# A two-layer hybrid trunk on one core: the recurrence's preparation in small pieces, a staging pool on the other side of memory, two right sides per step

## The chip, the cores and the metric

One core of one Trainium2 chip. The metric is the device time in microseconds of one execution. The engines are TensorE (PE; its weight loads are listed as PEld), VectorE (DVE), ScalarE (ACT), GpSimd (POOL) and SyncE (SP), which here only issues DMAs.

## The reference

Two layers over 1024 tokens of width 1024. Each is a token mixer, an MLP and a gated per-layer input, each behind an RMSNorm and added to the residual. The mixer of layer 0 is attention; that of layer 1 a recurrence (S5, complex and diagonal, 32 groups of 16 channels with 64 states) beside a short convolution. Cut to what matters here:

```python
for i in range(DEPTH):                          # DEPTH = 2
    hn = rms_norm(h, norm_mix[i])
    y = attention_mixer(hn, ...) if i % 2 == 0 else recurrent_conv_mixer(hn, ...)   # ends in "@ w_out"
    h = h + y
    hn = rms_norm(h, norm_mlp[i])
    h = h + jnp.square(jax.nn.relu(hn @ w_mlp_in[i])) @ w_mlp_out[i]    # 1024 -> 4096 -> 1024
    hn = rms_norm(h, norm_ple[i])
    h = h + (p[i] @ w_ple_proj[i]) * jax.nn.sigmoid(hn @ w_ple_gate[i])
return rms_norm(h, norm_final)

# in s5_mixer, from the parameters alone (the kernel's "preparation"):
abar_re, abar_im = mag * jnp.cos(li * dt), mag * jnp.sin(li * dt)
bb_re = coef_re[..., None] * br - coef_im[..., None] * bi
```

## The kernel before

**Products.** Every fp32 operand is split into a high part (ScalarE, L76) and the rest, the low part (VectorE, L79 for data, L89 for weights). `mm3` (L93) makes three matmuls of a product: L95 high × high, L96 low data × high weights (the names in the trace say `xl,wh`), L97 high data × low weights. `wtile` (L81) loads a raw block of weights `wr` (two buffers) on SP's queue and splits it into `wh` and `wl` (three buffers each). A matmul has 512 columns, half of the tokens.

**Order.** TensorE's instructions stand in the order of the program. On the other engines a scheduler sets the order by the program's order; each engine then works through its own row of instructions, and SP issues its DMAs one after the other.

**Layer 0's MLP up** (`mlp_up_plain`, L356). 32 blocks m of the hidden width, two halves n each, 24 matmuls a half. The first two blocks run together. When the first result is to be evicted, `rstd_full` makes the norm's scale from the statistics: its sums are two more matmul groups, copied out by VectorE as `rs_v` (L137). Then `out` (L361) evicts each half, scaled, into a tile `z` (VectorE, L370), and behind a full block ScalarE applies Relu and Square (L375, L376). For each pair of blocks `z_out` (L633) makes differences `tt` on VectorE (L642 to L645) and stores `z` (`oa`, `ob`, issued by ScalarE, L639, L640) and `tt` (`ot`, issued by GpSimd, L647) to the chip's memory. `z` and `tt` lie in a pool `cu`, on the left side of the on-chip memory.

**The recurrence's preparation** (`s5_prep`, a generator) needs only parameters, so it runs inside these 32 blocks, a piece at each of nine values of m:

```python
if m in (1, 5, 9, 12, 16, 19, 22, 25, 27):
    next(prep, None)
```

The first `next` runs the whole introduction (exponentials, sine and cosine, powers: many small VectorE operations on 128x32) and the first of eight "quads" (`s5_quad`: four groups each; products `Gt` and `CA`, tables `ct` and `st`). What a quad has for TensorE, four transposes (L1131) and four small matmuls, sits in `later`, run at the `next` after.

**Layer 0's MLP down** (`mlp_down`) opens a pool on the left, in the place where `cu` was. Its loads `raw` (weights, L668) and `zr` (the stored `z`, L674) alternate on SP's queue, and are split into `wh`, `wl`, `zh`, `zl`. The very first product is a lead (`down_lead`, operands `sh`, `sl`), loaded and split inside MLP up.

**Layer 1's output projection** (`out_proj_halves`, L409) runs left and right halves of the tokens apart, eight blocks m each. In the right half, at m = 1 and m = 2, four of the left half's rows of blocks each are normed (L465) and split (L79 into `x0l` to `x7l`): the right sides of the MLP that follows.

Of the kernel before, what the change touches and what calls it, by code (L numbers as in the profile page):

```python
# [13 lines left out]
ALU = mybir.AluOpType  # L14
# [51 lines left out]
class Trunk:  # L66
# [95 lines left out]
    def run(self):  # L162
        tc, nc, A = self.tc, self.nc, self.A
        pool = tc.tile_pool
        with pool(name="w", bufs=1, side=LEFT) as self.wp, \
# [11 lines left out]
            for l in range(2):  # L177
                if l == 0:
                    self.attention(xp)
                with pool(name=f"md{l}", bufs=6, space=PSUM, reuse_waits="tile") as self.mx, ExitStack() as rs:  # L180
# [4 lines left out]
                    if l == 0:  # L185
                        with pool(name=f"xu{l}", bufs=1, side=RIGHT, reuse_waits="tile") as xu:
                            hp = hs.enter_context(pool(name=f"h{l}", bufs=1, side=RIGHT, reuse_waits="tile"))
                            sp = self.ss.enter_context(pool(name=f"st{l}", bufs=1, side=RIGHT, reuse_waits="tile"))
                            xs, st = self.out_proj(l, xp, hp, xu, sp)
                            nxt.close()  # L190
                            with pool(name=f"cu{l}", bufs=1, side=LEFT, reuse_waits="tile") as cu:
                                first = self.mlp_up_plain(l, xs, st, cu, xu, hs)
# [163 lines left out]
    def mlp_up_plain(self, l, xs, st, cu, xu, hs):  # L356
# [5 lines left out]
        def out(m, n, ps):  # L362
            if not r:
                r.append(self.rstd_full(st, xu, cu))
                self.ss.close()
                hs.close()
            s = slice(n * H, n * H + H)
            if m not in z:
                z[m] = cu.tile([P, T], F32, tag="zp", bufs=4, name="z")
            nc.vector.tensor_tensor(z[m][:, s], ps, r[0][:, s], ALU.mult)  # L370
            if n:
                if m == FB - 1:
                    with self.tc.high_priority():
                        first.append(self.down_lead(l, self.s0))
                nc.scalar.activation(z[m], z[m], AF.Relu)  # L375
                nc.scalar.activation(z[m], z[m], AF.Square)  # L376
                if m % 2:
                    self.z_out(m // 2, z.pop(m - 1), z.pop(m), cu)
                if m in (1, 5, 9, 12, 16, 19, 22, 25, 27):
                    next(prep, None)  # L380

        with self.tc.tile_pool(name=f"s0{l}", bufs=1, side=LEFT, reuse_waits="tile") as self.s0:
# [26 lines left out]
    def out_proj_halves(self, l, xp, hp, sp, xa, X):  # L409
# [35 lines left out]
        for s in (lt, rt):  # L445
            for m in range(3 if s is lt else 0, KB):
# [8 lines left out]
                if s is rt and m in (1, 2):  # L455
                    for k in range(m * 4 - 4, m * 4):
                        self.norm_half(l, h, st, k, lt)
                        X[m, k % 4] = self.split(h[k][:, lt], xa, (f"x{k}h", f"x{k}l"), 1)
# [502 lines left out]
    def s5_prep(self):  # L961
# [4 lines left out]
        with tc.tile_pool(name="prep", bufs=1, side=LEFT, reuse_waits="tile") as pr:  # L966
# [16 lines left out]
            self.pexp(dt, ld, tmp)  # L983
            x = tmp()
            v.tensor_tensor(x, lr, dt, ALU.mult)
            self.pexp(mag, x, tmp)
            x = tmp()
            v.tensor_tensor(x, li, dt, ALU.mult)
            self.sincos(sn, cs, x, tmp)

# [19 lines left out]
            for t in range(8):  # L1010
                for j in range(2):
                    nc.scalar.copy(rv[j][:, t * G : (t + 1) * G], w(j, 7 - t))

# [14 lines left out]
            v.tensor_tensor(ci, ci, den, ALU.mult)  # L1028

# [16 lines left out]
            pend = None  # L1046
            for q in range(8):
                if pend:
                    pend()
                pend = self.s5_quad(q, pr, pw, rv, cr, ci, rot, sgn, nsgn)  # L1050
                yield
            pend()
# [11 lines left out]
    def s5_quad(self, q, pr, pw, rv, cr, ci, rot, sgn, nsgn):  # L1064
# [21 lines left out]

        def outer(out, tab, nt, X1, X2):
# [9 lines left out]
        outer(Gt, rv, 8, bb1, bb2)  # L1097
        CA = big("CA", 576)
        outer(CA, pw, 9, C1, C2)
        ca4 = CA.rearrange("p (g t c) -> p g t c", g=4, c=16)  # L1100
        cc = big("cc")
        nc.scalar.copy(cc.rearrange("p (g t c) -> p g t c", g=4, c=16), ca4[:, :, 1:9, :])
        self.spill(pr, q, 4, cc)

# [4 lines left out]
        for j in range(7):  # L1109
# [9 lines left out]
            v.tensor_tensor(s3[:, :, hi], s3[:, :, hi], m, ALU.add)  # L1119
        v.tensor_scalar(st, st, sgn, None, ALU.mult)  # L1120
# [3 lines left out]
        def later():  # L1124
            ps = self.bank()
            for g in range(4):
                nc.tensor.transpose(ps[:, g * P : g * P + P], Gt[:, g * P : g * P + P], self.ident)
            self.spill(pr, q, 2, ps)
            kp = self.bank()
            for g in range(4):  # L1130
                nc.tensor.matmul(kp[0:16, g * P : g * P + P], bb1[:, g * 16 : g * 16 + 16], ca4[:, g, 0:8, :], start=True, stop=True)  # L1131
            M = big("M")
            v.memset(M, 0.0)
            kt = big("kt")[0:16]
            nc.scalar.copy(kt, kp[0:16, :])
            k4 = kt.rearrange("p (g t c) -> p g t c", g=4, c=16)
            di = pr.tile([16, 64], F32, name="di", tag="di", bufs=1)
            v.tensor_tensor(g4(di), self.ident[0:16, 0:16].unsqueeze(1).to_broadcast([16, 4, 16]),
                            self.s5_dT[:, gs].unsqueeze(2).to_broadcast([16, 4, 16]), ALU.mult)
            v.tensor_tensor(k4[:, :, 0, :], k4[:, :, 0, :], g4(di), ALU.add)  # L1140
            m4 = M.rearrange("p (g t c) -> p g t c", g=4, c=16)
            for t in range(8):
                nc.sync.dma_start(m4[t * 16 : t * 16 + 16, :, t:8, :], k4[:, :, 0 : 8 - t, :])
            self.spill(pr, q, 0, M)
        return later
# [961 lines left out]
```

## Time and profile before

| | |
|---|---|
| median of three runs | 2575.11 us (2574.72 to 2578.71) |
| the profiled execution | 2579.28 us |
| its span in the trace | 2577.5 us |
| TensorE busy | 2486.7 us, 96% |
| VectorE busy | 1726.0 us, 67% |
| ScalarE busy | 1082.6 us, 42% |
| granted TensorE clock, mean | 0.985 |

The profiled execution is one of its own, apart from the three timed runs. All starts below are in microseconds from the start of its span. TensorE's share is high enough that the kernel's time is TensorE's work and the gaps in it. The clock is given in parts of 2.4 GHz.

### The profile page before, as it was taken

How to read it: one execution, taken by the hardware profiler on the slowest of the kernel's cores; microseconds unless marked ns; L12 is line 12 of the kernel's file. 1: busy time of each engine (PE TensorE's matmuls, PEld its weight loads, DVE VectorE, ACT ScalarE, POOL GpSimd, SP SyncE). 2: the span in 40 equal slices, each digit the busy share in tenths (PEclk: the TensorE clock that was granted, in tenths of full speed). 3: DMA queues.
4: the chain of work that ended last, by engine and by line, in shares of the span. 5: the costliest groups of instructions: out<-in, count | busy, mean ns of one | idle time of the engine just before them, and what ended most of it. 6: DMA issues, size and time to landing. Idle time of an engine off the chain costs nothing.

```text
span 2577.5 us, 33019 instructions
## 1 busy us (share of the span) xinstructions
PE 2486.7 (96%) x12104; PEld 2057.1 (80%) x12104; DVE 1726.0 (67%) x3189; ACT 1082.6 (42%) x1615; POOL 131.3 (5%) x128
## 2 busy tenths in 40 slices
PE   8999999979899999899999999999899999999998
PEld 6888898968687877688887897887688887888877
DVE  6776756554766776356776768665786664568776
ACT  5554555542333333343344432333554444333445
POOL 1111111000000000000000000000000000000000
PEclk9999999989999999999999999999999999999999
DMA  5443524264254555677853656354353447677552
GB/s 175 111 131 97 150 63 118 61 198 154 85 180 164 197 190 193 270 239 242 282 191 134 212 171 194 131 187 132 139 196 135 152 170 297 235 243 280 202 183 97
DMA packets 184754, 449.82 MB, mean 175 GB/s; under 512 B 24848, under 2 KB 56848, under 8 KB 184592
## 3 DMA queue, kind: packets, MB, share of 16 engines
q1 hardware_dynamic: 155904, 371.94, 43.8%
q0 software_dynamic: 12800, 46.14, 4.6%
q10 hardware_dynamic: 15888, 29.63, 3.1%
q8 instruction: 95, 1.56, 0.3%
q14 instruction: 67, 0.55, 0.1%
HBM read 297.55 MB, written 123.73 MB: 163 GB/s over the span
## 4 chain that ended last, share of the span: by engine, by line
PE 85%; DVE 8%; ACT 2%; issue 2%; DMA 1%; SPq 0%; DVEq 0%; ACTq 0%
PE mm L95 26%; PE mm L97 26%; PE mm L96 26%; PE tp L1927 2%; PE S L1894 1%; PE S L1895 1%; PE o L1952 1%; PE o L1951 1%; DVE zl L79 1%; DVE p L1897 1%; PE S L2019 1%; DVE wl L89 0%; DVE h L465 0%; DVE tl L79 0%; DVE p L1916 0%
## 5 line engine op out<-in xcount | busy, mean ns | idle before, releaser
L97 PE MATMUL mm<-xh,wl 128*128 128x512 f32 (+1 forms) x1504 | 583.9, 388 | 13.4 <-DVE st L1108 8.7
L95 PE MATMUL mm<-xh,wh 128*128 128x512 f32 (+1 forms) x1504 | 589.9, 392 | 0.3 <-ACT wh L76 0.3
L96 PE MATMUL mm<-xl,wh 128*128 128x512 f32 (+1 forms) x1504 | 580.8, 386 | 1.6 <-DVE xl L155 1.6
L95 PE MATMUL mm<-zh,wh 128*128 128x512 f32 x880 | 350.2, 398 | 8.5 <-ACT zh L76 8.5
L96 PE MATMUL mm<-zl,wh 128*128 128x512 f32 x880 | 350.1, 398 | 1.7 <-DVE zl L79 1.7
L97 PE MATMUL mm<-zh,wl 128*128 128x512 f32 x880 | 349.8, 397 | 0.0
L97 PEld LDWEIGHTS mm<-xh,wl 128*128 128x128 f32 x1504 | 284.5, 189 | 78.2 <-DVE st L1108 9.1
L96 PEld LDWEIGHTS mm<-xl,wh 128*128 128x128 f32 x1504 | 284.7, 189 | 61.4 <-DVE xl L155 2.0
L95 PEld LDWEIGHTS mm<-xh,wh 128*128 128x128 f32 x1504 | 284.6, 189 | 59.8 <-ACT sph L76 1.5
L76 ACT ACTIVATE wh<-wr 128x1024 fp32r<-128x1024 f32 (+1 forms) x137 | 143.8, 1052 | 446.1 <-PE mm L96 356.1
L95 PEld LDWEIGHTS mm<-zh,wh 128*128 128x128 f32 x880 | 166.4, 189 | 49.9 <-ACT zh L76 9.3
L96 PEld LDWEIGHTS mm<-zl,wh 128*128 128x128 f32 x880 | 166.4, 189 | 43.0 <-DVE zl L79 2.5
L97 PEld LDWEIGHTS mm<-zh,wl 128*128 128x128 f32 x880 | 166.3, 189 | 40.5
L76 ACT ACTIVATE wh<-raw 128x1024 fp32r<-128x1024 f32 x78 | 82.7, 1060 | 239.9 <-issue 117.0
L79 DVE TENSOR_TENSOR wl<-raw,wh 128x1024 fp32r<-128x1024 f32 x78 | 95.4, 1223 | 100.3 <-ACT wh L76 100.2
L89 DVE TENSOR_TENSOR wl<-wr,wh 128x1024 fp32r<-128x1024 f32 x98 | 119.6, 1222 | 59.6 <-ACT wh L76 59.3
L1902 ACT ACTIVATE p<-p,m 128x128 f32<-128x128 f32 (+7 forms) x128 | 99.1, 774 | 96.6 <-DVE m L1897 95.5
L79 DVE TENSOR_TENSOR zl<-zr,zh 128x1024 fp32r<-128x1024 f32 x110 | 134.1, 1219 | 2.4 <-ACT zh L76 2.2
L76 ACT ACTIVATE zh<-zr 128x1024 fp32r<-128x1024 f32 x110 | 115.0, 1045 | 0.7 <-DMA zr<-oa 0.7
L95 PE MATMUL mm<-wh,xh 128*128 128x256 f32 x384 | 112.6, 293 | 2.1 <-DVE v L1651 1.4
L97 PE MATMUL mm<-wh,xl 128*128 128x256 f32 x384 | 109.7, 286 | 0.0
L96 PE MATMUL mm<-wl,xh 128*128 128x256 f32 x384 | 109.6, 285 | 0.0
(680 smaller groups left out, 4476.2 us busy)
## 6 DMA issues: line engine op xcount, KB each, us to landing
raw<-w_m SPq DMA_DIRECT2D x158, 512.0 KB, 5.8
wr<-w_m SPq DMA_DIRECT2D x69, 512.0 KB, 4.1
ot<-tt POOLq DMA_DIRECT2D x64, 512.0 KB, 5.0
zr<-ot SPq DMA_DIRECT2D x64, 512.0 KB, 4.9
ob<-z ACTq DMA_DIRECT2D x32, 512.0 KB, 4.6
zr<-ob SPq DMA_DIRECT2D x32, 512.0 KB, 4.2
s<-s SPq DMA_DIRECT2D x64, 256.0 KB, 5.0
wr<-w_out SPq DMA_DIRECT2D x24, 512.0 KB, 3.5
```

The lines of the kernel that those rows point to most:

```text
L76: self.nc.scalar.activation(out, in_, AF.Copy, scale=scale)
L79: self.nc.vector.tensor_tensor(out, full, hi.bitcast(F32), ALU.subtract)
L89: self.weng.tensor_tensor(l, raw, h.bitcast(F32), ALU.subtract)
L95: mm(ps, L[0], R[0], start=first, stop=False)
L96: mm(ps, L[0], R[1], start=False, stop=False)
L97: mm(ps, L[1], R[0], start=False, stop=last)
L1894: nc.tensor.matmul(S, qh, qk["k"][c][:, k], start=True, stop=False)
L1895: nc.tensor.matmul(S, ql, qk["k"][c][:, k], start=False, stop=True)
L1897: nc.vector.tensor_tensor_reduce(pt[:, k], S, self.tab[:, T - w + k.start : T - w + k.stop], -0.125, m, ALU.add, ALU.min, m2)
L1902: nc.scalar.activation(pt[:, :w], pt[:, :w], AF.Exp, bias=m, scale=-1.0, accum_out=den)
L1927: nc.tensor.transpose(tps[:, off + n * P : off + n * P + P], maps[j][:, kb * P : kb * P + P], self.ident)
L1951: nc.tensor.matmul(oq, vv, th[:, q], start=first, stop=False)
```

## The change

Three edits, independent in the code.

1. `s5_prep` and `s5_quad` yield in 78 places: six in the introduction, nine in a quad. `out` calls `next` once behind the left and twice behind the right half of every block from m = 1. The quads' parts for TensorE now stand at m = 5, 8, 11, ... 26 (before: 5, 9, 12, ... 27), in the line of the quad itself.
2. The pool `cu` opens on the right side, behind the statistics, once the pools of the statistics (`st`) and of the residual (`h`) are closed; the temporaries of `rstd_full` go to the pool `s0` on the left.
3. In `out_proj_halves` two norms and splits stand at each of m = 1, 2, 3, 4.

```diff
-                            with pool(name=f"cu{l}", bufs=1, side=LEFT, reuse_waits="tile") as cu:
-                                first = self.mlp_up_plain(l, xs, st, cu, xu, hs)
+                            first = self.mlp_up_plain(l, xs, st, xu, hs)
...
-    def mlp_up_plain(self, l, xs, st, cu, xu, hs):
+    def mlp_up_plain(self, l, xs, st, xu, hs):
...
-                r.append(self.rstd_full(st, xu, cu))
+                r.append(self.rstd_full(st, xu, self.s0))
                 self.ss.close()
                 hs.close()
+                r.append(cs.enter_context(self.tc.tile_pool(name=f"cu{l}", bufs=1, side=RIGHT, reuse_waits="tile")))
+            cu = r[1]
...
-                if m in (1, 5, 9, 12, 16, 19, 22, 25, 27):
+            if m:
+                for _ in range(1 + n):
                     next(prep, None)
 
-        with self.tc.tile_pool(name=f"s0{l}", bufs=1, side=LEFT, reuse_waits="tile") as self.s0:
+        with self.tc.tile_pool(name=f"s0{l}", bufs=1, side=LEFT, reuse_waits="tile") as self.s0, ExitStack() as cs:
...
-                if s is rt and m in (1, 2):
-                    for k in range(m * 4 - 4, m * 4):
+                if s is rt and m in (1, 2, 3, 4):
+                    for k in range(m * 2 - 2, m * 2):
                         self.norm_half(l, h, st, k, lt)
-                        X[m, k % 4] = self.split(h[k][:, lt], xa, (f"x{k}h", f"x{k}l"), 1)
+                        X[k // 4 + 1, k % 4] = self.split(h[k][:, lt], xa, (f"x{k}h", f"x{k}l"), 1)
...
             self.pexp(dt, ld, tmp)
+            yield
             x = tmp()
             v.tensor_tensor(x, lr, dt, ALU.mult)
             self.pexp(mag, x, tmp)
+            yield
...
-            pend = None
+            yield
             for q in range(8):
-                if pend:
-                    pend()
-                pend = self.s5_quad(q, pr, pw, rv, cr, ci, rot, sgn, nsgn)
-                yield
-            pend()
+                yield from self.s5_quad(q, pr, pw, rv, cr, ci, rot, sgn, nsgn)
...
         outer(Gt, rv, 8, bb1, bb2)
+        yield
         CA = big("CA", 576)
         outer(CA, pw, 9, C1, C2)
+        yield
...
         self.spill(pr, q, 4, cc)
+        yield
...
+            if j in (2, 4):
+                yield
...
-        def later():
-            ps = self.bank()
-            for g in range(4):
-                nc.tensor.transpose(ps[:, g * P : g * P + P], Gt[:, g * P : g * P + P], self.ident)
-            self.spill(pr, q, 2, ps)
...
+        yield
+        ps = self.bank()
+        for g in range(4):
+            nc.tensor.transpose(ps[:, g * P : g * P + P], Gt[:, g * P : g * P + P], self.ident)
+        self.spill(pr, q, 2, ps)
+        kp = self.bank()
...
+        yield
+        M = big("M")
```

Lines of the changed kernel lie one or two further down from MLP up on, and more behind the new yields. Where instructions stand, at three places:

VectorE, layer 0's MLP up, around the low weights (L89) of blocks 3 and 4, before. `CA`, `ct`, `st`, `spl`, `om`, `rm` belong to the first quad, `rc` and `rs_76..` to the introduction; the two `rs_v` of the norm stand 63 and 61 rows ahead of the first L89:

```order
L1095 TENSOR_TENSOR CA<-CA,om 128x576
L1038 TENSOR_TENSOR rc_7670<-rc_7663 128x32
L1041 SCALAR_TENSOR_TENSOR rs_7671<-rc_7663,rs_7664 128x32
L1107 MEMSET ct 128x4
L1040 TENSOR_TENSOR rc_7670<-rc_7670,tiny 128x32
L370 TENSOR_TENSOR z<-mm,rstd 128x512
L1114 TENSOR_TENSOR ct<-ct,rc_7628 128x4
L370 TENSOR_TENSOR z<-mm,rstd 128x512
L79 TENSOR_TENSOR spl<-cc,sph 128x512
L89 TENSOR_TENSOR wl<-wr,wh 128x1024
L1108 MEMSET st 128x4
```

The same engine with the change:

```order
L1088 TENSOR_TENSOR bb_7780<-bb_7780,bc 128x64
L1047 TENSOR_TENSOR rc_7703<-rc_7703,tiny 128x32
L1046 TENSOR_TENSOR tiny<-rs_7704 128x32
L89 TENSOR_TENSOR wl<-wr,wh 128x1024
L137 TENSOR_SCALAR rs_v<-mm 128x512
L1045 TENSOR_TENSOR rc_7710<-rc_7703 128x32
L1048 SCALAR_TENSOR_TENSOR rs_7711<-rc_7703,rs_7704 128x32
L137 TENSOR_SCALAR rs_v<-mm 128x512
L1047 TENSOR_TENSOR rc_7710<-rc_7710,tiny 128x32
L1046 TENSOR_TENSOR tiny<-rs_7711 128x32
```

The first L89 has gone from behind the evictions and the first quad's `CA` to the row ahead of the first `rs_v`, in the middle of the introduction; the second L89 stands 35 rows behind that `rs_v`.

SP, from the last load of the gate's weights (`w_pg`) into the first loads of layer 0's MLP down, with the semaphores that each issue waits for, before. DMAHW5 of the first `raw` is the store of the last `ob`, its DVE the last `tt`, its Activation the last Square; DMASW are the stores of `ot`, issued by GpSimd:

```order
L83 DMA wr<-w_pg 128x1024 [waits DMAHW2_49,DVE_49]
L668 DMA raw<-w_m 128x1024 [waits DMAHW5_49,DMAHW6_49,DVE_49,Activation_49]
L674 DMA zr<-oa_184 128x1024 [waits DMAHW7_49]
L668 DMA raw<-w_m 128x1024 [waits DMASW7_49,DMASW5_49,DMAHW0_49,DMASW3_49,DMASW1_49]
L674 DMA zr<-oa_185 128x1024 [waits DMAHW1_49,PE_49]
```

With the change (DMAHW6 of the first `raw` is the `ob` store of block 27, its PE a matmul of the norm's statistics; DMAHW0 of the second a load of `w_pg`; the first `zr` waits for transfers and a matmul of the last quad):

```order
L83 DMA wr<-w_pg 128x1024 [waits DMAHW5_49,DMAHW2_49,DVE_49]
L670 DMA raw<-w_m 128x1024 [waits DMAHW6_49,PE_49]
L676 DMA zr<-oa_184 128x1024 [waits DMAHW3_49,DMAHW7_49,DMAHW1_49,PE_49]
L670 DMA raw<-w_m 128x1024 [waits DMAHW0_49]
L676 DMA zr<-oa_185 128x1024 [waits DMAHW4_49,DMAHW1_49]
```

The first `raw` no longer waits for the last `ob`, for VectorE or for ScalarE, and the second no longer for `ot`.

VectorE, layer 1's output projection, right half, from an eviction (L426) to the low weights (L89) of block 4, before:

```order
L426 TENSOR_TENSOR h<-mm,h 128x512
L79 TENSOR_TENSOR x4l<-h,x4h 128x512
L465 SCALAR_TENSOR_TENSOR h<-h,gains,rstd 128x512
L434 TENSOR_TENSOR acc<-acc,sq 128x512
L465 SCALAR_TENSOR_TENSOR h<-h,gains,rstd 128x512
L79 TENSOR_TENSOR x5l<-h,x5h 128x512
L465 SCALAR_TENSOR_TENSOR h<-h,gains,rstd 128x512
L79 TENSOR_TENSOR x6l<-h,x6h 128x512
L426 TENSOR_TENSOR h<-mm,h 128x512
L79 TENSOR_TENSOR x7l<-h,x7h 128x512
L89 TENSOR_TENSOR wl<-wr,wh 128x1024
```

With the change, the rows up to the same L89 (L428 is the eviction, L467 the norm, L436 the statistics):

```order
L467 SCALAR_TENSOR_TENSOR h<-h,gains,rstd 128x512 x3
L428 TENSOR_TENSOR h<-mm,h 128x512
L79 TENSOR_TENSOR x2l<-h,x2h 128x512
L79 TENSOR_TENSOR x3l<-h,x3h 128x512
L436 TENSOR_TENSOR acc<-acc,sq 128x512
L79 TENSOR_TENSOR x4l<-h,x4h 128x512
L467 SCALAR_TENSOR_TENSOR h<-h,gains,rstd 128x512
L89 TENSOR_TENSOR wl<-wr,wh 128x1024
```

The low weights of block 4 stand behind `x4l` now, no longer behind `x7l`: six rows fewer from the first eviction of the right half.

## Rows read from the trace of the kernel before

**Rows 1.** The page: its first line, and in part 1 the engines' busy time.

```profile
span 2577.5 us, 33019 instructions
...
PE 2486.7 (96%) x12104; PEld 2057.1 (80%) x12104; DVE 1726.0 (67%) x3189; ACT 1082.6 (42%) x1615; POOL 131.3 (5%) x128
```

**Rows 2.** Waits of TensorE: engine, line, what ended them, us in all, times, longest.

```profile
PE mm L97 <- DVE st L1108: 8.7, 1, 8.7
...
PE mm L95 <- ACT zh L76: 8.5, 2, 8.2
```

**Rows 3.** Windows: us, busy of PE, PEld, DVE, ACT, POOL; PE clock, DMA share, GB/s.

```profile
700.00:720.00 20.00, 14.81 (x53) 11.83 (x54) 18.66 (x74) 6.54 (x7) 0.00 (x0) 0.74 0.61 205
800.00:900.00 100.00, 100.00 (x440) 80.09 (x439) 73.18 (x233) 34.44 (x40) 5.80 (x8) 1.00 0.54 185
```

**Rows 4.** Timeline of VectorE: start us, length us, line, operation, output<-inputs, [idle before].

```profile
667.88 0.14 DVE L980 TENSOR_SCALAR nsgn<-sgn 128x1 f32<-128x1 f32 x1
...
682.90 0.18 DVE L1038 TENSOR_TENSOR tiny<-tiny 128x32 f32<-128x32 f32 x1
684.41 0.69 DVE L137 TENSOR_SCALAR rs_v<-mm 128x512 f32<-128x512 f32 x1 [1.32 <-PE mm L119]
...
689.71 0.69 DVE L370 TENSOR_TENSOR z<-mm,rstd 128x512 f32<-128x512 f32 x1
...
703.92 1.22 DVE L89 TENSOR_TENSOR wl<-wr,wh 128x1024 fp32r<-128x1024 f32 x1
```

**Rows 5.** Timeline of TensorE around 696 to 712 us.

```profile
696.11 0.39 PE L96 MATMUL mm<-xl,wh 128*128 128x512 f32 x1
705.19 0.80 PE L97 MATMUL mm<-xh,wl 128*128 128x512 f32 x1 [8.69 <-DVE st L1108]
...
710.48 0.40 PE L97 MATMUL mm<-xh,wl 128*128 128x512 f32 x1
...
711.88 0.40 PE L97 MATMUL mm<-xh,wl 128*128 128x512 f32 x1
```

**Rows 6.** Waits of SP's queue, 1000 to 1100 us.

```profile
SPq L668 <- DMA ob<-z: 26.0, 1, 26.0
```

**Rows 7.** Timeline of SP, from 1020 us.

```profile
1051.20 0.33 SPq L668 DMA_DIRECT2D raw<-w_m  x1
```

**Rows 8.** Timeline of ScalarE, from 1044 us.

```profile
1046.88 1.06 ACT L376 ACTIVATE z<-z 128x1024 f32<-128x1024 f32 x1
```

**Rows 9.** Timeline of VectorE, from 1044 us.

```profile
1049.19 0.69 DVE L645 TENSOR_TENSOR tt<-z,tt 128x512 f32<-128x512 f32 x1
...
1058.94 1.22 DVE L79 TENSOR_TENSOR zl<-zr,zh 128x1024 fp32r<-128x1024 f32 x1
```

**Rows 10.** Timeline of TensorE, 1048 to 1067 us.

```profile
1050.25 0.39 PE L97 MATMUL mm<-sh,wl 128*128 128x512 f32 x1
1058.84 0.80 PE L95 MATMUL mm<-zh,wh 128*128 128x512 f32 x1 [8.19 <-ACT zh L76]
...
1065.49 0.39 PE L96 MATMUL mm<-zl,wh 128*128 128x512 f32 x1
```

**Rows 11.** Timeline of VectorE, 1765 to 1786 us.

```profile
1771.48 0.68 DVE L426 TENSOR_TENSOR h<-mm,h 128x512 f32<-128x512 f32 x1
...
1784.60 1.22 DVE L89 TENSOR_TENSOR wl<-wr,wh 128x1024 fp32r<-128x1024 f32 x1
```

**Rows 12.** Timeline of TensorE, 1781 to 1790 us.

```profile
1782.73 0.40 PE L96 MATMUL mm<-xl,wh 128*128 128x512 f32 x1
1785.87 0.80 PE L97 MATMUL mm<-xh,wl 128*128 128x512 f32 x1 [2.74 <-DVE wl L89]
...
1789.03 0.42 PE L95 MATMUL mm<-xh,wh 128*128 128x512 f32 x1
```

**Rows 13.** Timeline of TensorE, 1838 to 1843 us.

```profile
1839.33 0.40 PE L97 MATMUL mm<-p1h,wl 128*128 128x512 f32 x1
1841.58 0.50 PE L95 MATMUL mm<-p0h,wh 128*128 128x512 f32 x1 [1.86 <-ACT ppo L496]
```

More of the change, by code (lines that the diff above doesn't have):

```diff
@@ L1103, in s5_quad @@
         self.spill(pr, q, 4, cc)
+        yield
         ct, st = big("ct"), big("st")
@@ L1119, in s5_quad @@
             v.tensor_tensor(s3[:, :, hi], s3[:, :, hi], m, ALU.add)
+            if j in (2, 4):
+                yield
         v.tensor_scalar(st, st, sgn, None, ALU.mult)
@@ L1122, in s5_quad @@
         nc.sync.dma_start(self.s5_d[q][7], st)
-        def later():
-            ps = self.bank()
-            for g in range(4):
-                nc.tensor.transpose(ps[:, g * P : g * P + P], Gt[:, g * P : g * P + P], self.ident)
-            self.spill(pr, q, 2, ps)
[L1129 to L1144, printed above, removed]
@@ L1145, in s5_quad @@
-        return later
+        yield
+        ps = self.bank()
[3 more added lines that the diff above has]
+        kp = self.bank()
+        for g in range(4):
+            nc.tensor.matmul(kp[0:16, g * P : g * P + P], bb1[:, g * 16 : g * 16 + 16], ca4[:, g, 0:8, :], start=True, stop=True)
+        yield
+        M = big("M")
+        v.memset(M, 0.0)
+        kt = big("kt")[0:16]
@@ new lines, in s5_quad @@
+        nc.scalar.copy(kt, kp[0:16, :])
+        k4 = kt.rearrange("p (g t c) -> p g t c", g=4, c=16)
+        di = pr.tile([16, 64], F32, name="di", tag="di", bufs=1)
+        v.tensor_tensor(g4(di), self.ident[0:16, 0:16].unsqueeze(1).to_broadcast([16, 4, 16]),
+                        self.s5_dT[:, gs].unsqueeze(2).to_broadcast([16, 4, 16]), ALU.mult)
+        v.tensor_tensor(k4[:, :, 0, :], k4[:, :, 0, :], g4(di), ALU.add)
+        m4 = M.rearrange("p (g t c) -> p g t c", g=4, c=16)
+        for t in range(8):
+            nc.sync.dma_start(m4[t * 16 : t * 16 + 16, :, t:8, :], k4[:, :, 0 : 8 - t, :])
@@ L1147, in recurrent @@
+        self.spill(pr, q, 0, M)
+        yield
     def recurrent(self, xp):
```

## The prediction

> **What bounds the kernel now.** I read the page's engine line first: TensorE is busy for 96% of the span, VectorE 67%, ScalarE 42% [rows 1]. TensorE takes its instructions in the order of the program, so a change that leaves its work alone can only win time in TensorE's gaps. The second view was therefore TensorE's waits. Most of its rows are spread over many short waits inside attention; two are single long ones, 8.7 us before a matmul of L97 and 8.2 of 8.5 us before one of L95 [rows 2]. I looked each one up in the timeline, together with the queue of the engine it waits for, and found a third place of the same kind. At all three the matmuls behind the gap start 0.43 us apart instead of 0.23: the clock has fallen from 2.4 to 1.2 GHz and comes back some 5 us later (in the 20 us around the first place the granted clock is 0.74 [rows 3]). So I charge a gap with more than its wait: I measure from the start at which the next matmul was due until full pace is back, and subtract what the matmuls started in between would have taken at full pace. Six starts after place 1 take 1.40 us [rows 5], 0.2333 us each; 24 of them, one half of a block of the MLP, take 5.6 us.
>
> **Place 1: low weights of block 3 (layer 0's MLP up).** *Before.* TensorE has started L96 of block 3 at 696.11, with the high weights, and needs the low ones at 696.34. VectorE computes these (L89) only at 703.92 [rows 4], with no idle time noted ahead of that row: it was busy with other work that stands in front. The waits table names the clearing of `st` (L1108) because that tiny row ended last; the operand is `wl`, 1.22 us long. What stands in front is `rs_v` (L137, 684.41) and 62 rows more, 19.5 us in all: the scale's arithmetic, evictions, and the recurrence preparation of the first quad, all of which one `next` puts there. *Cost.* L97 starts at 705.19 and full pace is back at 710.48 [rows 5]. That is 14.14 us from 696.34, in which 12 matmuls start (12 × 0.2333 = 2.80): 11.34 us lost.
>
> *After.* L89 of block 3 stands one row ahead of the first `rs_v` instead of 63 behind. In front of it now stand 24 more rows of the preparation than before stood ahead of `rs_v`. The preparation's first 118 rows run from 667.88 to 682.90 [rows 4], 0.13 us each, so these take about 3.1 us, and `wl` 1.2. VectorE idled 1.3 us just there, waiting for the statistics' sum. So `wl` ends near 687.3, nine us before it is needed. What is late next is `rs_v`, by some 2.9 us, and with it the first eviction `z`: 692.6 instead of 689.71 [rows 4]. It frees a bank for block 3, whose first matmul is at 695.9: 3 us spare. Block 4's `wl` stood one row behind block 3's and now stands 35 rows behind `rs_v`. By the share of rows it starts 10.8 us after 687.3 (63 took 19.5); at worst, if all waiting sits in those 35, it ends 19.5 + 1.2 us after, at 708.0. It is needed 11.2 us after block 3's, at 707.5. So the worst is half a microsecond late, the likely case 8 us early. I take the whole 11.34 us as gained.
>
> **The preparation later on.** TensorE's instructions for the eight quads (four transposes, four small matmuls) move by a block each and are the same in number, and VectorE has one row fewer in all. Between 800 and 900 us TensorE was busy for all 100 us with VectorE at 73% [rows 3]. Smaller pieces of the same work leave that share, and put fewer rows between an eviction and the `wl` behind it. I charge nothing; the cover is VectorE's free 27%. If it were gone, rival D says what that costs.
>
> **Place 2: from layer 0's MLP up to its MLP down.** *Before.* SP stands at the first `raw` load for 26.0 us [rows 6], until the last `ob` store has landed, because the new tiles of MLP down lie where the staging pool lay; it issues at 1051.20 [rows 7], so SP came there at about 1025. TensorE is out of work after 1050.25. It resumes at 1058.84 and is at full pace at 1065.49 [rows 10]: 15.01 us from 1050.48 with 13 starts (3.03), 11.97 us lost. *After.* The staging pool lies on the other side, over the residual tiles that are long dead, and the first load waits only for the `ob` store of block 27, two pairs before the last, and for an early matmul; the first `zr` also for the last quad's tables. So it can issue right behind the weight loads ahead of it, near 1025, and lands some 20 us before TensorE runs dry. The queues behind are not shortened, though: ScalarE splits `wh` and `zh` of the first step behind the last `Square` (1046.88, [rows 8]) and its store issue, so `zh` is there by about 1050.5. VectorE splits `wl` and `zl` behind the last `tt` (1049.19, [rows 9]): `wl` from 1049.8, `zl` from 1050.95 to 1052.2. So the first matmul starts on time or 0.1 us late, and the second, on `zl`, waits until 1052.2, about 1.6 us with what stands around it. Would the clock fall over that? After a gap of 2.25 us between starts (1839.33 to 1841.58) the rows go on at full pace [rows 13], after the 3.14 us of place 3 they don't. So I take 1.6 us as what remains, and 10.37 us as gained; the ends are 11.97 (nothing remains) and 6 (the wait is 3 us or more, and the clock goes with it, as in place 3).
>
> **Place 3: layer 1's output projection, right half.** *Before.* Four norms and splits stand at each of m = 1 and 2, and 21 VectorE rows, from the eviction at 1771.48, run back to back ahead of block 4's `wl` at 1784.60 [rows 11]: 0.625 us each. TensorE needs it at 1782.96, starts at 1785.87 and is at full pace at 1789.03 [rows 12]: 6.07 us with 7 starts (1.63), 4.43 us lost. *After.* Two norms and splits a step leave 15 rows ahead of it, 9.4 us: `wl` runs from 1780.9 to 1782.1, 0.9 us ahead of the need. One eviction among the 15 comes two rows earlier than it did, near 1777.1, when TensorE has just finished its block (5.6 us before 1782.5), and may wait some 0.3 us. Block 5's `wl` has the six rows that were taken away in front, and a block more time. I take 4.43 us as gained, the ends being 4.43 and nothing.
>
> **Where the staging lies.** The move puts tiles at other addresses; no row compares two places for one tile, so speeds could differ. The nearest rows, a `tt` in the pool (0.69 us, [rows 9]) and an eviction into `h` outside it (0.68 us, [rows 11]) are alike for the same shape: I charge nothing.
>
> **Sum.** 11.34 + 10.37 + 4.43 = 26.1 us. The profiled execution took 2579.28 us, span 2577.5 [rows 1], so it would take 2553.1; the median of the runs shown lies 4.2 us lower, so the forecast for the median is 2575.1 − 26.1 = 2549.0.
>
> The pace enters each loss. The Trainium skill, "TensorE: Matmul & The Clock Gate", section "Wait — 56ns, not 53.3ns?", has 215.7 ns from start to start for matmuls of 512 columns at 2.4 GHz, where the rows here have 233; at 1.2 GHz its 426.7 ns are the 0.43 us of the rows. An estimate by that page's pace would make the matmuls inside the three losses cheaper (32 × 0.0176) and the gain 0.6 us larger, 2548.4. The measurement decides, so it stays out of the sum.
>
> **Rivals.**
> *A. Place 3's margin fails.* 0.9 us, less the eviction's wait, is thin. If `wl` is still late by a few tenths, little comes back; if late by as much as before, all 4.4: 2553.4. For it: a late `rstd` chain ahead of 1771.48 shifts all 15 rows. Against: nothing in that chain is touched.
> *B. Place 2's wait is longer than 1.6 us,* because the splits run in another order or the loads come later, and the clock falls: 6 of the 10.4 us remain gained at the least that I reckon with, 2553.3; with the loads held back by a store after all, as before, nothing of it, 2559.4. Against the second: no store of the last pairs stands among the new waits of the first load.
> *C. Place 1's stall moves to block 4 or to the first evictions.* That takes VectorE 20 rows or more slower than I have it; price up to 11.3 us, 2560.3.
> *D. Slower than before: TensorE waits for the quads' own operands.* The small pieces leave a quad's last products (`CA`) closer to the matmuls that read them. It decides when a wait of about 3.3 us opens at each of the eight quads (26.1 / 8); with 4.43 us each, the price that place 3 shows for a 3.14 us gap, 8 × 4.43 = 35.4 and the time is 2584.4. Against: the reading matmuls stand a block or more behind, 11.2 us, and VectorE has its free quarter.
> *E. The loads of MLP down come so early that they take the staging's or the gate weights' bandwidth,* and nothing changes elsewhere: below 1 us, inside the range.
>
> **How the numbers follow.** My forecast 0.72; A 0.11, B 0.09, C 0.03, D 0.02, a gain under 0.2% by several of these together 0.03. The range goes from 2545 (nothing remains at place 2, −1.6; the pace of the page, −0.6; and the runs of before differ by up to 4 us, of which I take half) to 2561 (C). It holds all but D and the last case, and allows for what I have not seen. A measurement of this kernel can tell about 0.2%, 5.2 us, from no change: faster 0.95, same 0.03, slower 0.02. All of A to C stays faster than 2570.
>
> **What would show it.** Place 1: L89 of block 3 near 686 us, TensorE with no gap from 696 to 711, granted clock 1.00 there. Place 2, by then 11 us earlier: `raw` issued near 1014, a gap of 1 to 2 us near 1039, and the clock kept; if the first matmul waits for ScalarE instead, my order of splits is wrong. Place 3, near 1761: block 4's `wl` done some 0.9 us ahead of its matmul, and no 1.2 GHz stretch. A wait of L1137's transposes or L1141's matmuls would be D. VectorE's busy time stays within 1 us of 1726 in every case; TensorE's, whose gaps close and slow matmuls speed up, falls by a few us. The forecast is wrong above all if a wait that these stalls hid behind (another weight load, another bank) opens at one of the three places.

## The result and the profile after

| | before | changed |
|---|---|---|
| first measurement, medians | 2576.91 us (4 runs) | 2555.53 us (4 runs, 2552.39 to 2557.18) |
| ratio, 95% interval | | 0.9915 (0.9898 to 0.9933) |
| measured again, beside its parts | 2578.17 us (15 runs, 2571.49 to 2581.82) | 2553.21 us (4 runs, 2551.61 to 2554.54) |
| ratio, 95% interval | | 0.9903 (0.9889 to 0.9916) |
| profiled execution | 2579.28 us | 2557.18 us |

The kernel became faster by 21 to 25 us, inside the range and 4 to 6.5 us above the 2549.0 that was forecast. The engines have the same instructions, and nearly the same busy time as in [rows 1] (VectorE 1.4 us more, where the prediction allowed 1); the page of the changed kernel, its first line and the busy times:

```profile
span 2555.4 us, 33046 instructions
...
PE 2484.1 (97%) x12104; PEld 2055.6 (80%) x12104; DVE 1727.4 (68%) x3189; ACT 1082.5 (42%) x1615; POOL 131.3 (5%) x128
```

Three windows of 20 us with the three places (columns as in [rows 3]; the places now come some 2, 9.5 and 20 us away from where they were):

```profile
690.00:710.00 20.00, 20.00 (x87) 16.12 (x86) 19.13 (x52) 9.11 (x12) 1.68 (x2) 1.00 0.45 155
1030.00:1050.00 20.00, 18.94 (x80) 14.75 (x79) 10.81 (x12) 9.80 (x10) 1.45 (x2) 1.00 0.65 230
1755.00:1775.00 20.00, 20.00 (x87) 16.09 (x86) 17.21 (x24) 8.98 (x13) 1.63 (x3) 1.00 0.38 121
```

At places 1 and 3 TensorE is busy for all 20 us with 87 matmuls at full clock; at place 2 1 us is missing and the clock stays at 1.00. The timeline of VectorE at place 1 answers to [rows 4], TensorE's L97 below it to [rows 5]:

```profile
686.35 1.22 DVE L89 TENSOR_TENSOR wl<-wr,wh 128x1024 fp32r<-128x1024 f32 x1
687.48 0.68 DVE L137 TENSOR_SCALAR rs_v<-mm 128x512 f32<-128x512 f32 x1
...
692.90 0.68 DVE L371 TENSOR_TENSOR z<-mm,rstd 128x512 f32<-128x512 f32 x1
...
702.97 1.22 DVE L89 TENSOR_TENSOR wl<-wr,wh 128x1024 fp32r<-128x1024 f32 x1
```

```profile
697.91 0.39 PE L96 MATMUL mm<-xl,wh 128*128 128x512 f32 x1
698.14 0.39 PE L97 MATMUL mm<-xh,wl 128*128 128x512 f32 x1
```

The low weights of block 3 are computed 1.1 us ahead of the first `rs_v` and done at 687.6, ten us before L97 reads them; it starts 0.23 us behind L96, without a gap. The first `z` comes 3.2 us later than before; 1.8 of these are a shift of the whole trace from ahead of this place (below). Block 4's low weights (702.97) are done at 704.2, five us before they are needed (698.14 + 11.2).

Place 2, the queues in turn: SP, ScalarE, VectorE and TensorE (they answer to [rows 7 to 10]):

```profile
1015.67 0.38 SPq L670 DMA_DIRECT2D raw<-w_m  x1
```

```profile
1037.36 1.06 ACT L377 ACTIVATE z<-z 128x1024 f32<-128x1024 f32 x1
...
1039.07 1.06 ACT L76 ACTIVATE wh<-raw 128x1024 fp32r<-128x1024 f32 x1 [0.65 <-ACT z L377]
1040.04 1.05 ACT L76 ACTIVATE zh<-zr 128x1024 fp32r<-128x1024 f32 x1
```

```profile
1039.66 0.68 DVE L647 TENSOR_TENSOR tt<-z,tt 128x512 f32<-128x512 f32 x1
1040.27 1.22 DVE L79 TENSOR_TENSOR wl<-raw,wh 128x1024 fp32r<-128x1024 f32 x1
1041.40 1.22 DVE L79 TENSOR_TENSOR zl<-zr,zh 128x1024 fp32r<-128x1024 f32 x1
```

```profile
1040.72 0.39 PE L97 MATMUL mm<-sh,wl 128*128 128x512 f32 x1
1041.14 0.49 PE L95 MATMUL mm<-zh,wh 128*128 128x512 f32 x1
1042.67 0.50 PE L96 MATMUL mm<-zl,wh 128*128 128x512 f32 x1 [1.04 <-DVE zl L79]
1043.01 0.40 PE L97 MATMUL mm<-zh,wl 128*128 128x512 f32 x1
```

`raw` issues at 1015.67, 23 us ahead of the first split. What is left is the order on ScalarE and VectorE: `wh`, `zh` behind the last Square, `wl`, `zl` behind the last `tt`. TensorE starts 0.19 us late and waits once, for `zl`: 1.53 us between two starts.

Place 3, VectorE and TensorE (they answer to [rows 11, 12]):

```profile
1751.70 0.68 DVE L428 TENSOR_TENSOR h<-mm,h 128x512 f32<-128x512 f32 x1
...
1761.09 1.22 DVE L89 TENSOR_TENSOR wl<-wr,wh 128x1024 fp32r<-128x1024 f32 x1
```

```profile
1762.94 0.39 PE L96 MATMUL mm<-xl,wh 128*128 128x512 f32 x1
1763.18 0.40 PE L97 MATMUL mm<-xh,wl 128*128 128x512 f32 x1
```

`wl` ends at 1762.3, L97 reads it at 1763.18 without a wait.

**Where the time came from.** TensorE's instructions are the same in both kernels but for where the quads stand, so each matmul can be matched and its start compared. I give the shift of the same matmul, changed kernel minus before, worked out from the two timelines: just ahead of place 1 it is +1.8 us (the changed kernel is late, in attention, which the change does not touch), and behind it −9.5; behind place 2 −19.9; ahead of place 3 −19.8, behind it −24.2; at the end −22.7. So the places gave 11.35, 10.37 and 4.45 us, 26.2 in all, and some 3.5 us were lost outside them. One part of that loss can be seen where a gap of 2.25 us stands in both kernels [rows 13]; TensorE's timeline behind it in the changed kernel:

```profile
1814.92 0.39 PE L97 MATMUL mm<-p1h,wl 128*128 128x512 f32 x1
1817.17 0.50 PE L95 MATMUL mm<-p0h,wh 128*128 128x512 f32 x1 [1.86 <-ACT ppo L498]
...
1818.22 0.63 PE L96 MATMUL mm<-p1l,wh 128*128 128x512 f32 x1
...
1821.21 0.58 PE L97 MATMUL mm<-p1h,wl 128*128 128x512 f32 x1
1821.62 0.39 PE L95 MATMUL mm<-p0h,wh 128*128 128x512 f32 x1
```

The gap is the same, 2.25 us from start to start. Before, full pace went on behind it; here the starts are 0.43 us apart from 1818.22 to 1821.21, the lower clock. By the shifts ahead of it and behind it that costs 1.5 us.

### The profile page after: what moved, and what is told of

Its sections match the earlier page's. It is cut to its first block, busy times and chain, and to the rows that moved or that the text cites. A ratio compares the mean times of both kernels' runs of the same rounds, so it can differ in the third digit from the quotient of the medians.

```text
span 2555.4 us, 33046 instructions
## 1 busy us (share of the span) xinstructions
PE 2484.1 (97%) x12104; PEld 2055.6 (80%) x12104; DVE 1727.4 (68%) x3189; ACT 1082.5 (42%) x1615; POOL 131.3 (5%) x128
## 4 chain that ended last, share of the span: by engine, by line
PE 86%; DVE 7%; ACT 2%; issue 2%; DMA 1%; SPq 0%; DVEq 0%; ACTq 0%
PE mm L95 26%; PE mm L97 26%; PE mm L96 26%; PE tp L1938 2%; PE S L1905 1%; PE S L1906 1%; PE o L1963 1%; PE o L1962 1%; DVE zl L79 1%; PE S L2030 1%; DVE p L1908 1%; DVE tl L79 0%; DVE p L1927 0%; DVE wl L89 0%; DMA ql<-zl 0%
## 5 line engine op out<-in xcount | busy, mean ns | idle before, releaser
L95 PE MATMUL mm<-xh,wh 128*128 128x512 f32 (+1 forms) x1504 | 588.2, 391 | 0.2 <-ACT wh L76 0.2
L97 PE MATMUL mm<-xh,wl 128*128 128x512 f32 (+1 forms) x1504 | 582.4, 387 | 2.0 <-DVE wl L89 2.0
L96 PE MATMUL mm<-xl,wh 128*128 128x512 f32 (+1 forms) x1504 | 580.4, 386 | 1.5 <-DVE xl L155 1.5
L96 PE MATMUL mm<-zl,wh 128*128 128x512 f32 x880 | 349.1, 397 | 2.1 <-DVE zl L79 2.1
L95 PE MATMUL mm<-zh,wh 128*128 128x512 f32 x880 | 349.1, 397 | 0.3 <-ACT zh L76 0.3
L97 PE MATMUL mm<-zh,wl 128*128 128x512 f32 x880 | 348.9, 396 | 0.0
L97 PEld LDWEIGHTS mm<-xh,wl 128*128 128x128 f32 x1504 | 283.7, 189 | 65.3 <-DVE wl L89 2.4
L96 PEld LDWEIGHTS mm<-xl,wh 128*128 128x128 f32 x1504 | 284.0, 189 | 61.6 <-DVE xl L155 2.0
L95 PEld LDWEIGHTS mm<-xh,wh 128*128 128x128 f32 x1504 | 283.7, 189 | 59.9 <-ACT sph L76 1.5
L96 PEld LDWEIGHTS mm<-zl,wh 128*128 128x128 f32 x880 | 165.7, 188 | 43.1 <-DVE zl L79 2.8
L95 PEld LDWEIGHTS mm<-zh,wh 128*128 128x128 f32 x880 | 165.7, 188 | 41.5 <-ACT zh L76 1.2
L97 PEld LDWEIGHTS mm<-zh,wl 128*128 128x128 f32 x880 | 165.8, 188 | 40.3
L89 DVE TENSOR_TENSOR wl<-wr,wh 128x1024 fp32r<-128x1024 f32 x98 | 119.5, 1222 | 55.4 <-ACT wh L76 55.3
L95 PE MATMUL mm<-wh,xh 128*128 128x256 f32 x384 | 112.0, 292 | 2.1 <-DVE v L1662 1.4
L96 PE MATMUL mm<-wl,xh 128*128 128x256 f32 x384 | 108.8, 283 | 0.0
L97 PE MATMUL mm<-wh,xl 128*128 128x256 f32 x384 | 108.8, 283 | 0.0
```

Source lines behind the costliest of these rows:

```text
L89: self.weng.tensor_tensor(l, raw, h.bitcast(F32), ALU.subtract)
L95: mm(ps, L[0], R[0], start=first, stop=False)
L96: mm(ps, L[0], R[1], start=False, stop=False)
L97: mm(ps, L[1], R[0], start=False, stop=last)
```

## Experiments

Two theories were set against each other. The first: the three stalls are all that the change removes, each belongs to one edit, and the difference between 26 and 21 us is falls of the clock and small waits in stretches that are not touched. The second: something systematic gives some 4 us back.

**The whole again** (`e0_all`, the changed kernel).

> The changed kernel once more, beside its three parts on one chip. By the trace the three places gave back 11.35, 10.37 and 4.45 us, 26.2 in all, but the medians so far differ by 21.4. Theory 1 (the three stalls are all there is; the missing 4 to 5 us are falls of TensorE's clock and small waits in stretches that the change does not touch, which come and go from one execution to the next): 24 to 28 us faster than before over more runs, and the profile of this execution has other such stretches than the first one. Theory 2 (something systematic gives 4 us back, as loads that now come earlier or tiles at other addresses): 21 to 22 us again, with the same losses at the same places as in the first profile (1.9 us before 600 us, 1.8 us between 1815 and 1850 us).

**The preparation in pieces alone** (`e1_pieces`): on the kernel before, the yields of the diff and

```diff
-                if m in (1, 5, 9, 12, 16, 19, 22, 25, 27):
+            if m:
+                for _ in range(1 + n):
                     next(prep, None)
```

> The preparation in pieces alone. Theory 1: place 1's stall goes (11.3 us), places 2 and 3 keep theirs: 11.3 us faster than before, 2565.6 for a before of 2576.9. Theory 2: 4 us less than that if the pieces are what gives time back (VectorE's rows between evictions, the quads' own operands), so 7 us faster. If the staging's side were needed for place 1 too (the scale's temporaries lie elsewhere), a stall of several us would be left near 696 us.

**The staging's side alone** (`e2_side`): the pool `cu` opened on the right inside `out`, the scale's temporaries in `s0`.

```diff
-                r.append(self.rstd_full(st, xu, cu))
+                r.append(self.rstd_full(st, xu, self.s0))
...
+                r.append(cs.enter_context(self.tc.tile_pool(name=f"cu{l}", bufs=1, side=RIGHT, reuse_waits="tile")))
```

> The staging pool on the right side alone. Theory 1: place 2's stall shrinks from 11.97 to 1.6 us, place 1 and 3 keep theirs: 10.4 us faster than before. Theory 2: if the earlier loads or the other addresses are what gives time back, about 6 us faster, with the loss in stretches next to the move or behind it.

**Two right sides per step alone** (`e3_norms`).

```diff
-                if s is rt and m in (1, 2):
-                    for k in range(m * 4 - 4, m * 4):
+                if s is rt and m in (1, 2, 3, 4):
+                    for k in range(m * 2 - 2, m * 2):
```

> Two right sides per step alone. Theory 1: place 3's stall goes (4.4 us), which is within what a measurement of this kernel can tell: 2 to 6 us faster, and in the trace no gap in the right half of the output projection. Theory 2: nothing, if what is gained there is lost in the lead of the next MLP up (the same gap of 2.25 us before L95, behind which the clock fell in the changed kernel and did not in the kernel before).

Measured, against the 15 runs of before on the same chip:

| kernel | median, us | ratio (95%) | us faster |
|---|---|---|---|
| e0_all | 2553.21 | 0.9903 (0.9889 to 0.9916) | 25.0 (21.7 to 28.6) |
| e1_pieces | 2568.35 | 0.9961 (0.9947 to 0.9974) | 9.8 (6.7 to 13.7) |
| e2_side | 2564.98 | 0.9948 (0.9934 to 0.9962) | 13.2 (9.8 to 17.0) |
| e3_norms | 2574.11 | 0.9985 (0.9975 to 0.9994) | 4.1 (1.5 to 6.4) |

The times alone settle little, since runs of one kernel differ by up to 10 us. The shifts of the same matmul against the profiled execution of before do (us gained at each place; the last column is the shift at the end less the three places):

| profiled execution | place 1 | place 2 | place 3 | all else |
|---|---|---|---|---|
| changed kernel | 11.35 | 10.37 | 4.45 | −3.5 |
| e0_all | 11.33 | 10.38 | 4.44 | +1.2 |
| e1_pieces | 11.34 | 0.17 | 0.03 | −2.9 |
| e2_side | 2.99 | 10.37 | −0.11 | +4.8 |
| e3_norms | 0.64 | 0.47 | 4.44 | +1.7 |

Where an edit touches a place, the gain repeats to a few hundredths of a us, and each edit alone gives its place whole. All else runs from −3.5 to +4.8, with both signs, in kernels that share that code word for word; two executions of the changed kernel differ there by 4.7. So theory 1 holds for the three places, and theory 2 falls in its size: e0 lost nothing like 4 us. Of the two losses that theory 2 expected again, the one ahead of 600 us did not come back (e0 is 1.2 us early there), the other did, as 1.5 us behind the gap of [rows 13]. The gap of 2.25 us ahead of L95 on `p0h` stands in all eleven profiled executions that I have; the clock fell behind it in five (the changed kernel, e0, e4, e7, e9) and did not in six. All five are among the seven executions of kernels that hold the three edits, none among the four of the others; with so few, chance is not excluded, nor is a part of these 1.5 us that comes with the change. That the gap's length settles this, as I had read it from [rows 13], is wrong. What settles it is not shown here.

One thing in that table was not expected: e2 got back 3.0 us at place 1 as well. Its timeline there, TensorE and then VectorE:

```profile
691.67 0.39 PE L96 MATMUL mm<-xl,wh 128*128 128x512 f32 x1
697.59 0.80 PE L97 MATMUL mm<-xh,wl 128*128 128x512 f32 x1 [5.53 <-DVE wl L89]
```

```profile
681.49 0.68 DVE L137 TENSOR_SCALAR rs_v<-mm 128x512 f32<-128x512 f32 x1
...
696.32 1.22 DVE L89 TENSOR_TENSOR wl<-wr,wh 128x1024 fp32r<-128x1024 f32 x1
```

In e2, which moves the pool and puts the scale's temporaries into `s0` (the two were not run apart), 28 more rows of the preparation come ahead of `rs_v`, and L89 stands 35 rows behind it instead of 63: the wait is 5.53 us instead of 8.69. The two edits overlap there, so the three kernels' own places add up to some 29 by the trace, and the whole to 26.

**Which pieces matter** (`e7_intro_whole`): the changed kernel without the six yields of the introduction.

```diff
             self.pexp(dt, ld, tmp)
-            yield
             x = tmp()
...
             v.tensor_tensor(ci, ci, den, ALU.mult)
-            yield
```

> The changed kernel with the introduction of the preparation in one piece again (118 rows, 15 us) and only the quads in pieces. If the cutting of the quads is what removes place 1's stall (the introduction is done before the scale's statistics arrive, and hides there): no stall, the time of the changed kernel, 2553. If it is the cutting of the introduction, because with it whole the first quad's products are already ahead of block 3's low weights: L89 stands 35 rows behind the first rs_v, as in the kernel with the staging's side alone, where the wait was 5.5 us and 8.3 us were lost: 2561, 17 us faster than before.

Measured: 2562.66 us, ratio 0.9940 (0.9925 to 0.9954) to a before of 2577.29, 14.6 us faster. The trace has place 1 at 3.8 us gained, places 2 and 3 at 10.36 and 4.45. TensorE's timeline, and VectorE's:

```profile
695.64 0.39 PE L96 MATMUL mm<-xl,wh 128*128 128x512 f32 x1
701.51 0.79 PE L97 MATMUL mm<-xh,wl 128*128 128x512 f32 x1 [5.48 <-DVE wl L89]
```

```profile
685.48 0.69 DVE L137 TENSOR_SCALAR rs_v<-mm 128x512 f32<-128x512 f32 x1
...
700.23 1.22 DVE L89 TENSOR_TENSOR wl<-wr,wh 128x1024 fp32r<-128x1024 f32 x1
```

So cutting the quads does not remove the stall while the introduction is whole. In the changed kernel it is the cut introduction that keeps the first quad's products behind block 3's low weights. The opposite, the introduction cut and the quads whole, was not run, so it is not shown that the introduction's cuts alone would do.

**The cover** (`e6_double`, twice as many pieces a block) **and half a step there** (`e9_four`, four a block).

```diff
-                for _ in range(1 + n):
+                for _ in range(2 + 2 * n):
```

> The changed kernel with twice as many pieces of the preparation behind each half (two and four), so that it is done after 13 blocks instead of 26, and the quads' parts for TensorE stand 1.5 blocks apart. My cover is VectorE's free quarter. If it is what hides the pieces: three blocks (33.6 us) then ask VectorE for 2 x 15 + 10.5 = 40.5 us, so evictions and low weights fall behind, TensorE waits some 7 us for every three blocks over nine or ten blocks, with the clock 20 to 30 us, and the time is 2573 to 2583, near that of before; waits of TensorE for wl, for quads' operands or for banks show up between 700 and 820 us. If the order keeps the pieces behind the evictions and nothing else waits for them: within 5 us of the changed kernel.

> The changed kernel with four pieces a block instead of three (two behind each half), so the quads stand 2.25 blocks apart. In the changed kernel the second quad's CA ends at 747.0 and is read at 767.0, 20 us later; at six a block TensorE waited for CA at each quad. If the spare time shrinks with the distance between quads (33.6 us, now 25.2), some 10 us are left and TensorE waits for no quad; block 3's low weights stand 19 rows behind the first rs_v, in front of the first quad's CA, and are in time: no loss at place 1, the time of the changed kernel. If quads' operands come late as soon as VectorE has more than three pieces a block, waits of 1 to 3 us before L1141.

e6 took 2584.48 us, ratio 1.0027 (1.0015 to 1.0038): slower than before, though places 2 and 3 still gave their 10.37 and 4.45. TensorE's waits from 690 to 880 us, and the window of 700 to 800:

```profile
PE mm L1141 <- DVE ct L1115: 7.8, 3, 3.2
PE mm L1141 <- DVE CA L1100: 5.7, 4, 2.2
PE mm L97 <- DVE ct L1115: 5.5, 1, 5.5
PE mm L1137 <- DVE Gt L1100: 2.8, 1, 2.8
```

```profile
700.00:800.00 100.00, 86.06 (x363) 67.14 (x364) 88.11 (x309) 34.09 (x43) 6.04 (x8) 0.92 0.65 223
```

The time is a little above what I expected. No later eviction or low weight is waited for (the L97 row is place 1). TensorE waits at the quads themselves, for `CA` and `Gt` (the tiny L1115 is named where it ended last), 1 to 3 us each, often with the clock behind. Between 690 and 1030 us the kernel falls 21 us behind the one before, 32 behind the changed one, some 8 of them at place 1; the other 24 lie inside the 20 to 30 that the expectation had, and place 1 was not in it. That is rival D of the prediction, at twice the rate. At four pieces a block (e9, `range(2)`: 2552.11 us, one run) TensorE has no wait at all between 690 and 1000 us; the same window, with VectorE at 85%:

```profile
700.00:800.00 100.00, 100.00 (x451) 79.73 (x450) 84.67 (x291) 36.64 (x45) 5.82 (x8) 1.00 0.63 218
```

D starts between four and six pieces a block. Two things change on that way, the distance between the quads and VectorE's load, and the traces show that the load is not spare in e6. Its window has 363 matmuls and 88.1 us of VectorE, e9's at full pace 451: at that pace e6's rows would ask VectorE for some 109 of 100 us (an estimate from the two lines). The 88% are low only because TensorE waits. The spare time between the end of `CA` and the first matmul that reads it says the same. The second quad, in the changed kernel (VectorE, TensorE) and in e6 (TensorE):

```profile
746.28 0.75 DVE L1100 TENSOR_TENSOR CA<-CA,om 128x576 f32<-128x576 f32 x1
```

```profile
767.01 1.05 PE L1141 MATMUL mm<-CA,bb 128*16 128x128 f32 x8
```

```profile
732.04 1.68 PE L1141 MATMUL mm<-CA,bb 128*16 128x128 f32 x8 [2.23 <-DVE CA L1100]
```

In the changed kernel the spare time is 25.7 us at the first quad and 20.0 at each of the other seven. In e9 it is 9.6 and 10.1 at the first two and falls to between 3 and 7 at the last four. In e6 it is 9.3 at the first quad and below 0.1 at all the others, though the program puts the readers five pieces on, 0.83 of a block, at every quad. So the distance alone would have left some 9 us (0.83 × 11.2); VectorE has run late. Part of that is VectorE's own waits (2.6 us for a transfer, ahead of the second quad's `CA`), and how much each counts for was not separated.

**What is left at place 2** (`e4_two_leads`, then `e8_two_leads`): operands of the second product of MLP down loaded and split inside MLP up.

```diff
                         first.append(self.down_lead(l, self.s0))
+                        first.append(self.down_lead(l, self.s0, 1))
...
-        nc.sync.dma_start(raw, self.A["w_m2"][l * 32])
+        nc.sync.dma_start(raw, self.A["w_m2"][l * 32 + 4 * g])
```

> The changed kernel, with the operands of layer 0's second down product loaded and split inside MLP up like those of the first (a second lead: three more tiles in the pool of the scale's temporaries). What remained at place 2 in the changed kernel is a late zl: the second matmul starts 1.53 us behind the first, about 1.6 us in all. If that is all that is left there: no gap at place 2, 1.6 us less than the changed kernel, that is 26 to 28 us faster than before. If the early loads or splits get in the way of the last blocks of MLP up (a late wl of blocks 30 or 31, a late eviction): a gap there of a few us instead, and the same time as the changed kernel or more.

> The second lead again, now with the list of the products that follow it in step (the run before it took the second product twice and so shifted all that came after). No gap at place 2: the operands of the second product are split between the last evictions, and those of the third have 5.6 us more. 1.6 us less than the changed kernel at place 2 by the trace, 25 to 28 us faster than before in the times; against the changed kernel this is below what the times can tell, so the trace decides. If the early operands cost the last blocks of MLP up something, a gap there instead.

e4 took the second product twice and dropped the last, so it computes something else and its time (2553.31 us, 0.9901, 0.9884 to 0.9917) is no measure of this edit. e8 took 2549.97 us, ratio 0.9896 (0.9880 to 0.9913) to a before of 2578.69: 28.7 us faster. TensorE's timeline at place 2, from the second lead into the first product behind it:

```profile
1039.23 0.39 PE L97 MATMUL mm<-sh,wl 128*128 128x512 f32 x1
1039.46 0.40 PE L95 MATMUL mm<-zh,wh 128*128 128x512 f32 x1
1039.70 0.40 PE L96 MATMUL mm<-zl,wh 128*128 128x512 f32 x1
1039.93 0.39 PE L97 MATMUL mm<-zh,wl 128*128 128x512 f32 x1
```

No gap is left; the shift over place 2 is 11.96 us, the whole of the loss. Against the changed kernel that is 1.6 us by the trace; the times can't tell it (the two ratios' intervals overlap). This is the fastest version of the study.

## Why the prediction was right, and where it was off

**Place 1**: 11.34 forecast, 11.35 measured. Less the shift of 1.8 us, `wl` was done at 685.8 (forecast 687.3) and the first `z` came at 691.1 (692.6): the rows put ahead cost 1.5 us less than I had taken. Block 4's `wl`, with 0.5 us late as the worst, was five us early. The step that named "fewer rows between an eviction and the `wl` behind it" did not say which cut does it; e7 shows that the quads' cuts do not do it while the introduction is whole. Nor did the sum see that the second edit touches place 1 as well (3.0 us in e2).

**The cover**: I costed the pieces at nothing because VectorE has a free quarter. The cost was right, and e6 does not speak against the reason: it uses the quarter up, and then TensorE waits. What the prediction had too small is the room beside it: it put the readers a block or more behind `CA`, 11.2 us, and they stand 20 us behind (second quad: `CA` done at 747.0, read at 767.0). Rival D had the mechanism and its link to the cover: at six pieces a block it takes 24 us (32 less place 1's 8), 3 us a quad.

**Place 2**: 10.37 forecast, 10.37 measured, with 1.6 us left on `zl` as worked out, and `raw` at 1015.67, 1013.9 less the shift, where 1014 was forecast. That the clock would hold came true, but the reason was too strong: behind a gap of 2.25 us it can fall as well.

**Place 3**: 4.43 forecast, 4.45 measured; `wl` 0.9 us ahead as forecast. Of the rivals A, B, C and E none came.

**The pace**: the 215.7 ns from start to start in the Trainium skill's "TensorE: Matmul & The Clock Gate" (section "Wait — 56ns, not 53.3ns?") would have made the gain 0.6 us larger. The three places gave what the rows' 233 ns say, to 0.02 us.

**The time**: the weak step is the last of the sum, "the median of the runs shown lies 4.2 us lower". I took the profiled execution for a slow one and the three runs for the level. With 15 runs the median of before is 2578.2, and the profiled 2579.28 was ordinary. Of the 6.5 us by which the first median lies above the forecast, 1.8 are this base (2576.9 for 2575.1) and 4.7 a smaller gain; of the 4.2 us of the second, 3.1 and 1.1. The sum on the profiled execution's own time, 2553.1, is nearer to both medians (2555.5 and 2553.2), in part by luck: the changed kernel's own profiled execution took 2557.18. The rest is what comes and goes outside the three places, −3.5 to +6.0 us over these executions (e8 has the +6.0), for which the range allowed.

## What to carry to other kernels

When one engine works through a queue in order, look for the large block that a helper puts ahead of a small operand with a date: what counts is how many rows stand between, and cutting one block does little for the operand while another, uncut, brings the same rows forward (e7). A background task cut fine is hidden as long as its own readers stay far enough behind and the engine keeps up: set the engine's work for a block against the time that the block takes at full pace, since a busy share read while others wait looks too low. When a gain of some us is forecast from one profile, set it against that profile's own time, and measure parts by the shift of the same instruction in two traces: here it repeats to some hundredths of a us where run times scatter by 10.

## What the runs showed of the hardware

The same idle gap of 2.25 us on TensorE, with the same matmuls around it, was followed by the lower clock in five of eleven profiled executions, costing 1.5 us by the shifts, and by full pace in six. Runs of one program on one chip differ by up to 10 us (2571.49 to 2581.82); of the first four of the changed kernel the fastest (2552.39) has the highest mean clock, 0.991, the others 0.988 and 0.989. The clock records in the eleven traces go with it: outside the three places TensorE had the lower clock for 40 us (e8) to 60 us (the changed kernel, whose second execution, e0, has 43), and the time lost or won outside them follows, some 0.4 us for each us at the lower clock, with a correlation of 0.9. So such falls, in code that no edit touches, account for most of the scatter between these executions. For the runs without a trace, and so for the step from 21 us in the first four to 25 in the next, it fits their mean clocks and was not tested; why the clock falls in one execution and not in the next stays open.
